# First scale and shift by quarters of the features, and five products begun with them

## The chip, the cores and the metric

One core of a Trainium2 chip runs the whole program. The metric is the device time of one execution in microseconds, as a median of runs; the profile is one execution of its own. The engines are PE (matrix products), PEld (its weight loads), DVE, ACT and POOL (elementwise work), and SP, which issues most of the DMAs here. Each engine takes its own instructions strictly in the order in which they were built.

## The reference, cut to what matters

Two layers of a decoder, for 256 prompt tokens and 8 x 4 sample tokens (288 columns in all), 1024 features: retention, a gated feed-forward part, a gated delta mixer, a second feed-forward part. Before each stands a norm that is scaled and shifted by a vector computed from the condition c. Of all this the change touches the first scale and shift and the first products of retention:

```python
cs = jax.nn.silu(c.astype(jnp.float32))
for l in range(DEPTH):
    mod = cs @ p['w_ada'][l].astype(jnp.float32) + p['b_ada'][l].astype(jnp.float32)
    sh1, sc1, g1, sh2, sc2, g2 = jnp.split(mod, 6, axis=-1)
    h = ada_rmsnorm(x, p['norm_mix'][l], sh1, sc1)
    ...
    out, S = retention_mixer(h, pos0, s_ret[i], p['w_ret_in'][i], p['w_ret_out'][i])

def ada_rmsnorm(x, g, shift, scale):
    xf = x.astype(jnp.float32)
    xn = xf * lax.rsqrt(jnp.mean(xf * xf, axis=-1, keepdims=True) + EPS) * g.astype(jnp.float32)
    return (xn * (1.0 + scale[:, None, :]) + shift[:, None, :]).astype(x.dtype)

def retention_mixer(h, pos0, s0, w_in, w_out):
    proj = jnp.einsum('btd,de->bte', h, w_in).astype(jnp.float32)
    ...
```

## The kernel before, in words

Features lie on partitions: x is 8 tiles (KT) of 128 features by 288 columns. Every product is made exact by splitting: a weight block of 128 x 1024 is loaded raw, ACT casts it to `whi` (line 414), DVE subtracts to get `wlo` (line 415); the normed features are split in the same way into `hh` and `hl`. A product of one output block (`product`, line 533) is then 8 tiles x 3 pairs (whi with hh, whi with hl, wlo with hh), 24 matmuls of 288 columns.

The condition's vectors need `w_ada`, 14 chunks of 8 loads each (512 KB a load). One load is four matmuls into `adaP` (line 453), each with a weight of 32 columns in a quarter of PE's columns. After a chunk's last load ACT copies adaP to `adaev` (line 459), PE transposes that twice into `adaT`, and DVE adds the bias and writes `mod` (line 466). `modulated` (line 601 on) turns mod into features: DVE makes the scale `am` (line 607), the sample columns `hs` in three steps (617, 621, 625), and for each feature tile `h` (631); ACT writes `hh` (626, 632); DVE and POOL write `hl` (634, 627). `rb`, the root of the mean square of each token, comes from PE and DVE beforehand (`token_rsqrt`).

All loads stand in one list, `plan_weights`, and SP issues them in that order as buffers come free: 8 of the pool `more0` and 4 of `raw` in the first phase. At the start the list is chunk 0 (8 loads), one retention weight `wri`, four loads of chunk 1, `wri`, four more, `wri`. Chunk 0 holds shift and scale of the first 512 features, chunk 1 of the others. `first_h` takes chunk 0, makes the first four tiles of features, and begins EARLY = 3 retention products with them, in banks that rotate (`mmt`), chunk 1 between them; the last one (LATE = 1) is begun after the second half's `modulated`. Then the three products get their second half. While `hold` is set, weights of the next phase are not cast. `proj` hands out the begun products first. A scheduling layer orders each engine's instructions, so the code's order is not the order of the program.

`load_cst` loads a table on ACT's queue, behind a POOL copy that reads `mod`, so that it starts no earlier than that column of mod exists.

Of the kernel before, what the change touches and what calls it, by code (L numbers as in the profile page):

```python
# [6 lines left out]
F32 = mybir.dt.float32  # L7
# [3 lines left out]
ALU = mybir.AluOpType  # L11
# [62 lines left out]
EARLY = 3  # L74
LATE = 1
# [115 lines left out]
def lay_out(inp):  # L191
# [8 lines left out]
    wa = np.concatenate([inp["w_ada"][0], inp["w_ada"][1], inp["w_ada_final"]], 1)  # L200

    wa[:, : 2 * DM] = wa[:, : 2 * DM].reshape(DM, 2, 2, 512)[:, ::-1].transpose(0, 2, 1, 3).reshape(DM, 2 * DM)
    d["wada"] = wa.reshape(KT, P, 14, 1024).transpose(2, 0, 1, 3).reshape(14 * KT, P, 1024)
# [90 lines left out]
class Program:  # L294
# [12 lines left out]
    def plan_weights(self):  # L307
        A = self.A
        ada = lambda ch: [("ada", ch, k, A["wada"][ch * KT + k]) for k in range(KT)]
# [12 lines left out]

        second, step = ada(1), -(-KT // (EARLY - LATE))
        plan = [ada(0)]
        for i in range(EARLY):
            plan[0] += wl("wri", i, 1) + second[i * step : (i + 1) * step]
# [120 lines left out]
    def ada_step(self, ch, k, r):  # L447
        nc = self.nc
        if k == 0:
            self.adaP = self.aux("adaP", self.ada_tag)  # L450
        rv = r.rearrange("p (c g f) -> p c g f", c=2, g=4)
# [5 lines left out]
        if k == KT - 1:  # L457
            ev = self.tmp.tile([P, T], F32, tag="t288", name="adaev", bufs=T288)[:, 0:256]
            nc.scalar.copy(ev, self.adaP[:, 0:256])
            pt = self.aux("adaT")  # L460
            for c in range(2):
                nc.tensor.transpose(pt[:, c * P : (c + 1) * P], ev[:, c * P : (c + 1) * P], self.ident)
            pt = pt[:, 0:256].rearrange("p (m r) -> p m r", r=32)[:, :, 0:9]
            for m, m0, n in ((0, 8 + 4 * ch, 4), (4, 4 * ch, 4)) if ch < 2 else ((0, 8 * ch, 8),):
                bias = self.prm("bada")[:, m0 : m0 + n].unsqueeze(2).to_broadcast([P, n, 9])
                nc.vector.tensor_tensor(self.mod[:, m0 : m0 + n, :], pt[:, m : m + n], bias, ALU.add)
# [134 lines left out]
    def modulated(self, norm, sh, sc, name, hi, lo=None, rb=None, m0=0, m1=KT):  # L601

        nc = self.nc
        n, ms = m1 - m0, slice(m0, m1)
# [30 lines left out]
        self.ada_due(FILLS[2])  # L635
# [9 lines left out]
    def first_h(self, rc):  # L645

        nc = self.nc
        h = self.h_tiles("ret")
        self.ada_due(4)
        rb = self.now(self.token_rsqrt(self.ssum, 1.0 / DM, "ret"))  # L650
        self.ada_due()
        self.load_cst(rc, "cst_a", nc.scalar, self.mod[:, 8, 0:1])
        self.modulated(0, 0, 1, "ret", *h, rb, 0, KT // 2)
        begun = []
        self.hold = True
        for i in range(EARLY):
            if i == EARLY - LATE:
                self.ada_due()
                self.modulated(0, 0, 1, "ret", *h, rb, KT // 2, KT)
            w = self.weights("wri")  # L660
            begun.append((self.mmt(f"pe{i}")[:, 0:T], w))
            self.product(*begun[-1], KT, 0, P, h, 0, KT // 2)
        if not LATE:
            self.ada_due()
            self.modulated(0, 0, 1, "ret", *h, rb, KT // 2, KT)
        self.load_cst(rc, "cst_r", nc.scalar, self.mod[:, CST_AT, 0:1])
        self.load_cst(self.cp, "cst_b", nc.scalar, self.mod[:, CST_AT, 0:1])
        self.load_cst(self.cp, "prm_b", nc.scalar, self.mod[:, CST_AT, 0:1])
        for i, (p, w) in enumerate(begun):
            if i == FREE:  # L670
                self.hold = False
            self.product(p, w, KT, 0, P, h, KT // 2)
        self.hold = False
        self.begun = [p for p, _ in begun]
        return h
# [1054 lines left out]
```

## Time and profile before

| what | us |
|---|---|
| median of 3 runs (1228.85 to 1232.32) | 1230.46 |
| the profiled execution's own time | 1235.09 |
| its span | 1233.3 |
| PE busy | 1162.4 |
| DVE busy | 877.2 |
| ACT busy | 608.4 |
| DMA moved, mean 218 GB/s | 269.08 MB |

Mean granted clock of PE over the span: 0.978. The span runs from the first to the last instruction; the execution's own time is 1.8 us longer. Times within the profile are microseconds from the span's start. A matmul's duration runs from its start until its last column is out, and the next one starts before that, so the pace is read from starts or from the chain, not from durations.

### The profile page before, as it was taken

To read this page: it belongs to the slowest core of one execution; us is meant where nothing else is said; L and a number is where in the kernel's file an instruction comes from. 1 tells how busy PE (TensorE), PEld (TensorE's weight loads), DVE (VectorE), ACT (ScalarE), POOL (GpSimd) and SP (SyncE) were. 2 spreads that over 40 slices of the span, in tenths; PEclk is the share of its full clock that TensorE was granted. 3 is DMA by queue.
4 is the path that set the end of the run, shared out by engine and by line. 5 is a ranking of instruction groups with operands and counts; after the bars stand their busy time and mean duration, and the time that the engine had idled before them with its cause. 6 is when DMAs were issued, how large, how long until landed. Compare 5 with 4: busy or idle time off the path is not lost.

```text
span 1233.3 us, 24974 instructions
## 1 busy us (share of the span) xinstructions
PE 1162.4 (94%) x9486; PEld 1045.2 (85%) x9486; DVE 877.2 (71%) x2038; ACT 608.4 (49%) x1258; POOL 326.0 (26%) x504
## 2 busy tenths in 40 slices
PE   6999999999999999999889888988899899999996
PEld 2879788797969999997777777977789699999996
DVE  3657574765766666667769888797965687878785
ACT  2444534344446445543674655745544365555542
POOL 0214142151301221233242124243222212233241
PEclk9999999999999999999989998999999899999997
DMA  9999696866689556556636652534334997878521
GB/s 350 347 335 331 224 338 230 315 239 236 226 298 400 196 161 199 171 181 243 219 84 209 218 165 61 161 129 120 126 109 130 307 358 257 258 238 264 182 76 39
DMA packets 97480, 269.08 MB, mean 218 GB/s; under 512 B 26816, under 2 KB 28832, under 8 KB 97232
## 3 DMA queue, kind: packets, MB, share of 16 engines
q1 hardware_dynamic: 87456, 234.42, 56.6%
q0 software_dynamic: 8032, 29.16, 6.3%
q10 hardware_dynamic: 1872, 3.90, 0.9%
q8 instruction: 75, 1.23, 0.4%
q14 instruction: 45, 0.37, 0.1%
HBM read 236.06 MB, written 31.39 MB: 217 GB/s over the span
## 4 chain that ended last, share of the span: by engine, by line
PE 77%; DVE 13%; ACT 3%; DMA 3%; issue 2%; POOL 1%; ACTq 0%; POOLq 0%; DVEq 0%
PE down L533 17%; PE fg L533 12%; PE fv L533 11%; PE pg L533 4%; PE pv L533 4%; PE adaP L453 4%; PE p L533 3%; PE gv L533 2%; PE gz L533 2%; DVE mp L1319 2%; DVE wlo L415 2%; PE gk L533 2%; PE pO L884 1%; PE pU L903 1%; PE pS L854 1%
## 5 line engine op out<-in xcount | busy, mean ns | idle before, releaser
L415 DVE TENSOR_TENSOR wlo<-more,whi 128x1024 fp32r<-128x1024 f32 x138 | 171.1, 1241 | 80.6 <-ACT whi L414 67.8
L414 ACT CAST whi<-more 128x1024 fp32r<-128x1024 f32 x138 | 144.4, 1048 | 139.6 <-PE down L533 53.3
L414 ACT CAST whi<-raw 128x1024 fp32r<-128x1024 f32 x123 | 128.0, 1044 | 146.3 <-PE down L533 44.1
L415 DVE TENSOR_TENSOR wlo<-raw,whi 128x1024 fp32r<-128x1024 f32 x123 | 154.2, 1256 | 60.6 <-ACT whi L414 36.5
L702 POOL TENSOR_TENSOR x<-x,dt 128x32 f32<-128x32 f32 x159 | 103.1, 649 | 138.9 <-DVE dt L700 137.2
L698 DVE SCALAR_TENSOR_TENSOR x<-down,mod,x 128x256 f32<-128x256 f32 x160 | 76.7, 479 | 52.5 <-PE down L533 51.9
L580 POOL TENSOR_TENSOR fal<-cv,fah 128x288 fp32r<-128x288 f32 x44 | 41.2, 936 | 217.3 <-ACT fah L579 186.3
L533 PE MATMUL down<-fal,whi 128*128 128x288 f32 x352 | 64.5, 295 | 0.0
L533 PE MATMUL down<-fah,whi 128*128 128x288 f32 x352 | 62.2, 294 | 0.0
L533 PE MATMUL down<-fah,wlo 128*128 128x288 f32 x352 | 62.1, 294 | 0.0
L904 DVE SCALAR_TENSOR_TENSOR S<-S,pU 128x512 f32<-128x512 f32 x64 | 42.2, 684 | 24.5 <-PE pU L903 24.4
L533 PE MATMUL fg<-hh_ffn,whi 128*128 128x288 f32 x352 | 58.4, 298 | 0.8 <-ACT hh_ffn L626 0.7
L533 PE MATMUL fv<-hh_ffn,whi 128*128 128x288 f32 x352 | 58.7, 297 | 0.0
L533 PE MATMUL fg<-hh_ffn,wlo 128*128 128x288 f32 x352 | 55.0, 296 | 0.0
L533 PE MATMUL fv<-hh_ffn,wlo 128*128 128x288 f32 x352 | 54.7, 295 | 0.0
L533 PE MATMUL fv<-hl_ffn,whi 128*128 128x288 f32 x352 | 54.2, 295 | 0.0
L533 PEld LDWEIGHTS fg<-hh_ffn,whi 128*128 128x128 f32 x352 | 50.3, 188 | 4.6 <-ACT hh_ffn L632 2.2
L533 PE MATMUL fg<-hl_ffn,whi 128*128 128x288 f32 x352 | 54.0, 295 | 0.0
L533 PEld LDWEIGHTS down<-fal,whi 128*128 128x128 f32 x352 | 52.4, 188 | 0.4 <-issue 0.4
L533 PEld LDWEIGHTS down<-fah,whi 128*128 128x128 f32 x352 | 51.9, 188 | 0.8 <-ACT whi L414 0.8
L533 PEld LDWEIGHTS fv<-hh_ffn,whi 128*128 128x128 f32 x352 | 50.3, 188 | 2.5 <-ACT ftail L934 1.2
L533 PEld LDWEIGHTS down<-fah,wlo 128*128 128x128 f32 x352 | 51.9, 188 | 0.0
(467 smaller groups left out, 2921.3 us busy)
## 6 DMA issues: line engine op xcount, KB each, us to landing
more<-in_wu SPq DMA_DIRECT2D x73, 512.0 KB, 5.2
raw<-in_wada SPq DMA_DIRECT2D x69, 512.0 KB, 4.8
raw<-in_wgi SPq DMA_DIRECT2D x48, 512.0 KB, 3.9
more<-in_wada SPq DMA_DIRECT2D x43, 512.0 KB, 6.3
more<-in_wd SPq DMA_DIRECT2D x36, 512.0 KB, 3.8
S<-in_sr SPq DMA_DIRECT2D x16, 1024.0 KB, 8.5
out_rs<-S POOLq DMA_DIRECT2D x16, 1024.0 KB, 6.9
raw<-in_wri SPq DMA_DIRECT2D x28, 512.0 KB, 4.6
```

The source lines that it names most:

```text
L414: nc.scalar.copy(hi[:, :c], r)
L415: nc.vector.tensor_tensor(lo[:, :c], r, hi[:, :c].bitcast(F32), ALU.subtract)
L453: nc.tensor.matmul(self.adaP[32 * g : 32 * g + 32, 0:256], lhsT=self.cs[:, k, :], rhs=rv[:, :, g, :], start=(k == 0), stop=(k == KT - 1), ...
L533: self.nc.tensor.matmul(out, lhsT=av[:, k, c0 : c0 + m], rhs=b[:, k, :], start=(k0 == 0 and i == 0), stop=(k1 == kts and i == len(seq) - 1))
L580: (nc.gpsimd if pool_lo else nc.vector).tensor_tensor(lo, src, hi.bitcast(F32), ALU.subtract)
L698: nc.vector.scalar_tensor_tensor(xm[:, :TP], p[:, :TP], g[:, 0:1], xm[:, :TP], ALU.mult, ALU.add)
L702: (nc.vector if gate == 11 and last and m == KT - 1 else nc.gpsimd).tensor_tensor(xv, xv, t, ALU.add)
L854: nc.tensor.matmul(pS, lhsT=kt[:, j, c * P : (c + 1) * P], rhs=vt[:, j, :], start=(j == 0), stop=(j == 1))
L884: nc.tensor.matmul(pO4[32 * g : 32 * g + 32, :], lhsT=qm[:, c, 4 * bb + g, :], rhs=S[bb, c][:, g, :], start=(bb == 0 and c == 0), stop=Fal ...
L903: nc.tensor.matmul(pU, lhsT=kms[g][:, c * P : (c + 1) * P], rhs=vst, start=True, stop=True)
L904: nc.vector.scalar_tensor_tensor(S[bb, c][:, g, :], S[bb, c][:, g, :], gamma4, pU, ALU.mult, ALU.add)
L1319: nc.vector.tensor_tensor(m, Ti[:, 0:k, :].rearrange("p j c -> p c j").unsqueeze(1).to_broadcast([P, w, 8, k]), X[:, 0:k, i:k].rearrange(" ...
```

## The change

The first 2048 columns of w_ada are laid out anew, in four quarters of 256 features. A quarter is four loads of 512 KB, each with two of the eight blocks of the contraction, and holds the quarter's shift and scale. A load is now eight matmuls of 128 columns instead of four of 256 (`ada_quarter`), and one transpose follows each quarter instead of two each half. The list of loads is: quarter 0, one `wri`, quarter 1, one, quarter 2, two, quarter 3, one. `first_h` goes by quarters: modulation and two feature tiles of the quarter, then the next two tiles of all products begun so far, then FIRST_W = (1, 1, 2, 1) new products over all tiles there are. Five products are begun instead of three, in five banks named in START_TAGS; the pool of the start holds five split weights instead of three. Bytes and matmul columns stay the same in sum.

```diff
-EARLY = 3
-LATE = 1
+FIRST_W = (1, 1, 2, 1)
+EARLY = sum(FIRST_W)
+START_TAGS = ["c", "mm", "s", "mm", "e"]
...
-    wa[:, : 2 * DM] = wa[:, : 2 * DM].reshape(DM, 2, 2, 512)[:, ::-1].transpose(0, 2, 1, 3).reshape(DM, 2 * DM)
-    d["wada"] = wa.reshape(KT, P, 14, 1024).transpose(2, 0, 1, 3).reshape(14 * KT, P, 1024)
+    d["wada"] = wa[:, 2 * DM :].reshape(KT, P, 12, 1024).transpose(2, 0, 1, 3).reshape(12 * KT, P, 1024)
+    w = wa[:, : 2 * DM].reshape(4, 2, P, 2, 4, 256)[:, :, :, ::-1]
+    d["wadq"] = w.transpose(4, 0, 2, 1, 3, 5).reshape(16, P, 1024)
...
-        second, step = ada(1), -(-KT // (EARLY - LATE))
-        plan = [ada(0)]
-        for i in range(EARLY):
-            plan[0] += wl("wri", i, 1) + second[i * step : (i + 1) * step]
+        plan = [[]]
+        for q, n in enumerate(FIRST_W):
+            plan[0] += [("ada", q - 4, k, A["wadq"][4 * q + k]) for k in range(4)]
+            plan[0] += wl("wri", sum(FIRST_W[:q]), n)
...
+    def ada_quarter(self, q, k, r):
+        nc = self.nc
+        rv = r.rearrange("p (a g f) -> p a g f", a=2, g=4)
+        for a in range(2):
+            for g in range(4):
+                nc.tensor.matmul(
+                    self.adaP[32 * g : 32 * g + 32, 0:P], lhsT=self.cs[:, 2 * k + a, :], rhs=rv[:, a, g, :],
+                    start=(k == 0 and a == 0), stop=(k == 3 and a == 1), skip_group_check=True,
+                )
...
-        self.ada_due(4)
-        rb = self.now(self.token_rsqrt(self.ssum, 1.0 / DM, "ret"))
-        self.ada_due()
-        self.load_cst(rc, "cst_a", nc.scalar, self.mod[:, 8, 0:1])
-        self.modulated(0, 0, 1, "ret", *h, rb, 0, KT // 2)
...
+        for q, n in enumerate(FIRST_W):
             self.ada_due()
-            self.modulated(0, 0, 1, "ret", *h, rb, KT // 2, KT)
...
+            if q == 0:
+                rb = self.now(self.token_rsqrt(self.ssum, 1.0 / DM, "ret"))
+            if q == 2:
+                self.load_cst(rc, "cst_a", nc.scalar, self.mod[:, 2, 0:1])
+            self.modulated(0, 0, 1, "ret", *h, rb, 2 * q, 2 * q + 2)
...
+            for i, (p, w) in enumerate(begun):
+                if q == 3 and i == FREE:
+                    self.hold = False
+                self.product(p, w, KT, 0, P, h, 2 * q, 2 * q + 2)
+            for i in range(n):
+                w = self.weights("wri")
+                begun.append((self.aux(f"pe{len(begun)}", START_TAGS[len(begun)])[:, 0:T], w))
+                self.product(*begun[-1], KT, 0, P, h, 0, 2 * q + 2)
```

The order of the instructions moves on every engine. Three places follow; names are tiles, with a number where it tells two of a kind apart.

DVE, from the last modulation of the start (`mod`) to the first split of features (`hl`). Before:

```order
L466 TENSOR_TENSOR mod<-adaT,prm 128x36 x2
L607 SCALAR_TENSOR_TENSOR am_ret<-mod,prm 128x36
L617 TENSOR_TENSOR hs_ret<-x,am_ret 128x128
L621 TENSOR_TENSOR hs_ret<-hs_ret,rb_ret 128x128
L631 SCALAR_TENSOR_TENSOR h_ret<-x,am_ret,rb_ret 128x256
L415 TENSOR_TENSOR wlo<-more_203,whi 128x1024
L625 TENSOR_TENSOR hs_ret<-hs_ret,mod 128x128
L631 SCALAR_TENSOR_TENSOR h_ret<-x,am_ret,rb_ret 128x256 x3
L634 SCALAR_TENSOR_TENSOR hl_ret<-h_ret,mod,hh_ret 128x256 x4
```

Now, the last quarter:

```order
L491 TENSOR_TENSOR mod<-adaT,prm 128x18 x2
L632 SCALAR_TENSOR_TENSOR am_ret<-mod,prm 128x18
L418 TENSOR_TENSOR wlo<-more_273,whi 128x1024
L642 TENSOR_TENSOR hs_ret<-x,am_ret 128x64
L646 TENSOR_TENSOR hs_ret<-hs_ret,rb_ret 128x64
L656 SCALAR_TENSOR_TENSOR h_ret<-x,am_ret,rb_ret 128x256
L650 TENSOR_TENSOR hs_ret<-hs_ret,mod 128x64
L656 SCALAR_TENSOR_TENSOR h_ret<-x,am_ret,rb_ret 128x256
L418 TENSOR_TENSOR wlo<-more_275,whi 128x1024
L659 SCALAR_TENSOR_TENSOR hl_ret<-h_ret,mod,hh_ret 128x256 x2
```

The last modulation now covers 2 tiles instead of 4; the split of a weight (`wlo`) stands right behind the scale `am`, ahead of the sample columns and of the first tile `h`, where it stood behind the first `h`; that weight, `more_273`, belongs to the next phase.

PE and ACT around the last modulation now (before, twelve matmuls of the third product followed the transpose, and one cast followed the copy `adaev`). PE:

```order
L558 MATMUL pe_437<-hl_ret,whi 128x288 x6
L558 MATMUL pe_437<-hh_ret,wlo 128x288 x6
L479 MATMUL adaP<-more_235,c 32x128 x7
L479 MATMUL adaP<-raw,c 32x128 x8
L479 MATMUL adaP<-more_259,c 32x128 x8
L558 MATMUL pe_556<-hh_ret,whi 128x288 x3
L487 MATMUL adaT<-cst,adaev 128x128
L558 MATMUL pe_556<-hh_ret,whi 128x288 x3
L458 MATMUL adaP<-raw,c 32x256 x4
L558 MATMUL pe_241<-hh_ret,whi 128x288
```

ACT:

```order
L417 CAST whi<-more_269 128x1024
L417 CAST whi<-more_271 128x1024
L485 COPY adaev<-adaP 128x128
L417 CAST whi<-more_273 128x1024
L417 CAST whi<-more_275 128x1024
L657 ACTIVATE hh_ret<-h_ret,mod 128x256
L651 CAST hh_ret<-hs_ret 128x2x32
L657 ACTIVATE hh_ret<-h_ret,mod 128x256
```

The last quarter's loads (`adaP` of 128 columns) come behind the second-quarter parts of four products; six matmuls of the fifth product (`pe_556`), the transpose and the first load of the next chunk (`adaP` of 256 columns) stand before the first matmul on the new tiles (`pe_241`). ACT has two casts of next-phase weights ahead of the copy and two between it and `hh`.

ACT at the start of the first feed-forward part, where `fg` and `fv` are gate and value blocks and `cv` is the gate's convolution. Before:

```order
L932 ACTIVATE cv<-fg_3981,prm_b 128x288
L933 COPY fhalo<-fg_3981 128x32
L934 COPY ftail<-fg_3981 128x2
L414 CAST whi<-raw 128x1024 x2
L932 ACTIVATE cv<-fg_4055,prm_b 128x288
L933 COPY fhalo<-fg_4055 128x32
L934 COPY ftail<-fg_4055 128x2
L414 CAST whi<-more_3953 128x1024
L939 ACTIVATE cv<-cv 128x288 x2
L414 CAST whi<-more_3955 128x1024
```

Now:

```order
L956 ACTIVATE cv<-fg_4073,prm_b 128x288
L957 COPY fhalo<-fg_4073 128x32
L958 COPY ftail<-fg_4073 128x2
L417 CAST whi<-raw 128x1024
L963 ACTIVATE cv<-cv 128x288
L956 ACTIVATE cv<-fg_4147,prm_b 128x288
L957 COPY fhalo<-fg_4147 128x32
L958 COPY ftail<-fg_4147 128x2
L604 CAST fah_4041<-cv 128x288
L417 CAST whi<-more_4043 128x1024
L963 ACTIVATE cv<-cv 128x288
```

The cast of the weight of the second value block was the second of the two `raw` casts, ahead of the second gate block's `cv`; it is now the cast of `more_4043`, behind that block's four ACT instructions and the rounding `fah`.

## Rows read from the trace of the kernel before

**Rows 1.** The page: busy time by engine; shares of the chain that ended last.

```profile
PE 1162.4 (94%) x9486; PEld 1045.2 (85%) x9486; DVE 877.2 (71%) x2038; ACT 608.4 (49%) x1258; POOL 326.0 (26%) x504
...
PE 77%; DVE 13%; ACT 3%; DMA 3%; issue 2%; POOL 1%; ACTq 0%; POOLq 0%; DVEq 0%
```

**Rows 2.** Windows, 46:340 us: busy time (count) by engine, PEclk, DMA share, GB/s.

```profile
46.00:340.00 294.00, 293.89 (x2169) 253.54 (x2169) 186.79 (x332) 129.29 (x223) 85.76 (x104) 1.00 0.77 276
```

**Rows 3.** Timeline of PE: start, us, what, shapes, count [idle before <- releaser].

```profile
11.87 1.08 PE L453 MATMUL adaP<-more,c 128*32 128x256 f32 x8 [0.20 <-DMA more<-in_wada]
13.15 1.06 PE L453 MATMUL adaP<-more,c 128*32 128x256 f32 x2 [0.20 <-DMA more<-in_wada]
14.14 1.44 PE L558 MATMUL st_ret<-ones,ssum 128*128 128x1 f32 x6
...
17.81 1.49 PE L564 MATMUL rb_ret<-cst,tr_ret 128*128 128x128 f32 x6 [0.37 <-DVE tr_ret L550]
...
25.56 0.40 PE L533 MATMUL pe<-hh_ret,whi 128*128 128x288 f32 x1 [2.44 <-ACT hh_ret L626]
...
51.82 1.23 PE L533 MATMUL pv<-hh_ret,whi 128*128 128x288 f32 x8
...
57.42 1.07 PE L453 MATMUL adaP<-raw,c 128*32 128x256 f32 x16
```

**Rows 4.** Windows of the start.

```profile
20.00:52.00 32.00, 27.07 (x202) 19.65 (x195) 21.03 (x45) 12.76 (x20) 5.97 (x11) 0.95 0.92 350
22.80:25.50 2.70, 0.32 (x8) 0.00 (x0) 2.63 (x8) 0.80 (x2) 0.05 (x1) 1.00 0.64 153
26.20:29.50 3.30, 3.30 (x21) 1.26 (x16) 2.64 (x6) 2.15 (x4) 0.00 (x0) 0.50 1.03 415
```

**Rows 5.** Waits of PE, 0:52 us: us in total, times, longest.

```profile
PE adaT L462 <- ACT adaev L459: 1.0, 2, 0.5
...
PE pe L533 <- DVE wlo L415: 0.9, 1, 0.9
PE pe L533 <- ACT whi L414: 0.5, 1, 0.5
```

**Rows 6.** Chain of waits in order of time: start, us, what.

```profile
48.78 4.79 PE pv L533 x36
```

**Rows 7.** Forms by tile: count, ns min/median/max, first and last start us, shapes.

```profile
L453 PE MATMUL adaP<-more,c x96: 379/634/637, 7.9 to 35.4; 128*32 128x256 f32 x96
...
L892 PE MATMUL pO<-vr,ats x32: 272/273/296, 82.6 to 301.1; 128*32 128x128 f32 x32
```

**Rows 8.** Timeline of ACT, start of the program.

```profile
21.23 0.37 ACT L459 COPY adaev<-adaP 128x256 f32<-128x256 f32 x1 [11.95 <-PE adaP L453]
21.50 1.05 ACT L414 CAST whi<-raw 128x1024 fp32r<-128x1024 f32 x1
...
23.88 0.51 ACT L632 ACTIVATE hh_ret<-h_ret,mod 128x256 fp32r<-128x256 f32 x1 [1.33 <-DVE h_ret L631]
```

**Rows 9.** Timeline of DVE, start of the program.

```profile
22.61 0.20 DVE L607 SCALAR_TENSOR_TENSOR am_ret<-mod,prm 128x36 f32<-128x36 f32 x1
...
23.37 0.47 DVE L631 SCALAR_TENSOR_TENSOR h_ret<-x,am_ret,rb_ret 128x256 f32<-128x256 f32 x1
...
38.11 1.22 DVE L415 TENSOR_TENSOR wlo<-more,whi 128x1024 fp32r<-128x1024 f32 x1
```

**Rows 10.** Timeline of SP's queue: the issue of the second retention weight.

```profile
23.19 0.33 SPq L400 DMA_DIRECT2D raw<-in_wri  x1
```

**Rows 11.** Timelines of ACT and PE, start of the first feed-forward part.

```profile
367.10 0.59 ACT L932 ACTIVATE cv<-fg,prm_b 128x288 f32<-128x288 f32 x1 [2.10 <-PE fg L533]
...
367.77 1.05 ACT L414 CAST whi<-more 128x1024 fp32r<-128x1024 f32 x1
...
370.87 0.43 ACT L579 CAST fah<-cv 128x288 fp32r<-128x288 f32 x1
...
367.99 1.32 PE L533 MATMUL fv<-hh_ffn,whi 128*128 128x288 f32 x8
```

More of the change, by code (lines that the diff above doesn't have):

```diff
@@ L308, in plan_weights @@
         A = self.A
-        ada = lambda ch: [("ada", ch, k, A["wada"][ch * KT + k]) for k in range(KT)]
+        ada = lambda ch: [("ada", ch, k, A["wada"][(ch - 2) * KT + k]) for k in range(KT)]
         wl = lambda name, i0, n: [("w", name, 0, A[name][i]) for i in range(i0, i0 + n)]
@@ L450, in ada_step @@
             self.adaP = self.aux("adaP", self.ada_tag)
+        if ch < 0:
+            return self.ada_quarter(ch + 4, k, r)
         rv = r.rearrange("p (c g f) -> p c g f", c=2, g=4)
@@ L463, in ada_step @@
             pt = pt[:, 0:256].rearrange("p (m r) -> p m r", r=32)[:, :, 0:9]
-            for m, m0, n in ((0, 8 + 4 * ch, 4), (4, 4 * ch, 4)) if ch < 2 else ((0, 8 * ch, 8),):
-                bias = self.prm("bada")[:, m0 : m0 + n].unsqueeze(2).to_broadcast([P, n, 9])
-                nc.vector.tensor_tensor(self.mod[:, m0 : m0 + n, :], pt[:, m : m + n], bias, ALU.add)
+            m0, n = 8 * ch, 8
+            bias = self.prm("bada")[:, m0 : m0 + n].unsqueeze(2).to_broadcast([P, n, 9])
+            nc.vector.tensor_tensor(self.mod[:, m0 : m0 + n, :], pt, bias, ALU.add)
+    def ada_quarter(self, q, k, r):
[7 more added lines that the diff above has]
+                )
+        if k == 3:
+            ev = self.tmp.tile([P, T], F32, tag="t288", name="adaev", bufs=T288)[:, 0:P]
+            nc.scalar.copy(ev, self.adaP[:, 0:P])
+            pt = self.aux("adaT")
+            nc.tensor.transpose(pt[:, 0:P], ev, self.ident)
+            pt = pt[:, 0:P].rearrange("p (m r) -> p m r", r=32)[:, :, 0:9]
+            for m, m0 in ((0, 8 + 2 * q), (2, 2 * q)):
+                bias = self.prm("bada")[:, m0 : m0 + 2].unsqueeze(2).to_broadcast([P, 2, 9])
+                nc.vector.tensor_tensor(self.mod[:, m0 : m0 + 2, :], pt[:, m : m + 2], bias, ALU.add)
     def spawn(self, gen):
@@ L603, in modulated @@
         nc = self.nc
-        n, ms = m1 - m0, slice(m0, m1)
+        n, ms, rb_given = m1 - m0, slice(m0, m1), rb
         am = self.tmp.tile([P, KT, 9], F32, tag="am", name=f"am_{name}", bufs=2)[:, 0:n]
@@ L634, in modulated @@
                 nc.vector.scalar_tensor_tensor(lo[:, m, :TP], h, shift[:, i, 0:1], hi[:, m, :TP].bitcast(F32), ALU.add, ALU.subtract)
-        self.ada_due(FILLS[2])
+        if rb_given is None:
+            self.ada_due(FILLS[2])
     def h_tiles(self, name):
@@ L648, in first_h @@
         h = self.h_tiles("ret")
-        self.ada_due(4)
-        rb = self.now(self.token_rsqrt(self.ssum, 1.0 / DM, "ret"))
-        self.ada_due()
-        self.load_cst(rc, "cst_a", nc.scalar, self.mod[:, 8, 0:1])
-        self.modulated(0, 0, 1, "ret", *h, rb, 0, KT // 2)
         begun = []
         self.hold = True
-        for i in range(EARLY):
-            if i == EARLY - LATE:
-                self.ada_due()
-                self.modulated(0, 0, 1, "ret", *h, rb, KT // 2, KT)
[L660 to L663, printed above, removed]
-            self.ada_due()
[L665 to L672, printed above, removed]
+        rb = None
+        for q, n in enumerate(FIRST_W):
+            self.ada_due()
+            if q == 0:
[3 more added lines that the diff above has]
+            self.modulated(0, 0, 1, "ret", *h, rb, 2 * q, 2 * q + 2)
+            if q == 3:
+                self.load_cst(rc, "cst_r", nc.scalar, self.mod[:, CST_AT, 0:1])
+                self.load_cst(self.cp, "cst_b", nc.scalar, self.mod[:, CST_AT, 0:1])
+                self.load_cst(self.cp, "prm_b", nc.scalar, self.mod[:, CST_AT, 0:1])
+            for i, (p, w) in enumerate(begun):
[6 more added lines that the diff above has]
+                self.product(*begun[-1], KT, 0, P, h, 0, 2 * q + 2)
         self.hold = False
```

## The prediction

> **What bounds the kernel now.** I read the page's totals and chain first: PE is busy 94% of the span and is 77% of the chain that ended last [rows 1]. The windows say where it is not: between 46 and 340 us PE stands still for 294.00 - 293.89 = 0.11 us [rows 2]. Whatever the start loses or gains therefore reaches 340 us undiminished, and the question is when PE gets there with the same work behind it. The change rewrites the first 50 us, so I read PE's timeline there. Two points matter: PE's first product on the normed features, at 25.56, and 51.82, when five products (two of the query, two of the key, one of the value of head 0) and all sixteen modulation loads are done [rows 3]. Between 20 and 52 PE is busy 27.07 of 32.00 us [rows 4]; most of the missing 4.93 us stands in five waits: 2.44 for the first half's features [rows 3], 1.0 for the copies of the two halves' modulation, 0.5 for a weight's cast and 0.9 for a wlo, both in the second half [rows 5]. DMA is full there (share 0.92) [rows 4], but PE's last wait for a load ends at 13.15 [rows 3]: from there on the order of ACT, DVE and PE bounds, not the loads.
>
> **The change, step by step.** Prices at full clock: a fp32r product of 288 columns 0.133 us (36 in 4.79) [rows 6], a modulation load 0.5 us (16 records, two loads, in 1.07) [rows 3].
>
> *A load in eight products of 128 columns instead of four of 256.* The trace has no such product of adaP. Bounds: the same time, since the columns are the same in sum, or twice it, if each product cost as much as a wide one: 1.0 us, 4.5 us more over the nine loads that fall after PE's first product. The nearest row is pO<-vr,ats, the same 32 x 128 shape: 273 ns from start to end against 379 for 256 columns, so the columns carry the difference [rows 7]. I take 0.5 us.
>
> *The first quarter.* Its fourth load is read out at 11.87 + 1.08 = 12.95 [rows 3]. ACT now has the cast of the first retention weight ahead of the copy of adaP; that weight is the fifth load, and the fifth load of before is first read at 13.15 [rows 3]. So: cast 1.05 to 14.2, copy 0.37 to 14.6 [rows 8], one transpose at the start's slow clock some 0.35 to 14.95, the token sums 1.44 to 16.4, the root 2.23 (from 15.58 to 17.81 before) [rows 3] with two small DVE steps of 0.2 between to 19.0, its broadcast 1.49 to 20.5 [rows 3], the small step and one tile 0.2 + 0.47, the rounding 0.5 [rows 8, 9]. PE's first product comes at 21.7 instead of 25.56.
>
> *What PE still has to do.* Before, from 25.56: seven loads 3.5, two transposes 0.44, 120 products 16.0: 19.9 us. It took 51.82 - 25.56 = 26.26. Of the 6.3 us more, the three waits of the second half are 1.9 (half of the 1.0, 0.5 and 0.9) [rows 5]; the stretch 26.20 to 29.50 ran at a granted clock of 0.50, after one in which PE was busy 0.32 of 2.70 us [rows 4], and lost half of 3.3, 1.65; 2.8 us are short stops and changes of weights. Now, from 21.7: nine loads 4.5, three transposes 0.7, the same 120 products 16.0, and one load of the next modulation chunk that the order now has ahead of the end, 0.5: 21.7 us.
>
> *PE's waits.* They come from ACT and DVE taking their work in order.
> Quarter 1: the second weight's cast stands behind the copy (0.37 + 1.05); PE has three products and a transpose, 0.6: it waits 0.8. The features' second tile stands behind a wlo of 1.22 [rows 9]; PE has four products and two loads: 1.1.
> Quarter 2: 0.6 for copy and transpose, 0.9 and 0.35 for the casts of the third and fourth weight, which stand behind the copy one after the other, 1.0 for the features, which stand behind both casts: 2.85.
> Quarter 3: this is the largest. Copy 0.37, transpose 0.3, two additions and the scale 0.5: 1.2. Then DVE's row is a wlo of a weight of the next phase, whose cast ACT starts only after the copy: it can start at 0.37 + 1.05 = 1.45 and ends at 2.7. Two small steps 0.4, a tile 0.47, its rounding 0.5: 4.1 us from the last load to PE's first product on the last two tiles. PE has six products of the fifth block, the transpose and that one load, 1.45: it waits 2.7.
> After the last product the next one takes the bank of the first, and waits until DVE has read that twice: 0.5.
> Sum 8.0 us (0.8 + 1.1 + 2.85 + 2.7 + 0.5 = 7.95), against 1.9 before.
>
> *Sum at the start.* 21.7 + 21.7 + 8.0 + the same 2.8 of short stops + 1.65 if a stretch runs at half clock as before = 55.9, or 54.2 without. Before it is 51.82 + 0.5 for the same work, 52.3. So 3.6 us later, or 1.9. I take the half clock, since two of the waits, 0.8 and 1.1, fall where it fell before. The Trainium skill (TensorE: Matmul & The Clock Gate, the section on the HAM clock gate) says that slow is the default state and that activity releases it; no run here shows yet whether products from 21.7 on are enough. By that rule PE's earlier start would keep the full clock and the sum at the start would be 1.9; the granted clock of before agrees in this, that it fell behind the idle stretch and rose again behind the busy one [rows 4].
>
> *Loads.* Bytes are the same. The fifteenth load waits until PE has read the ninth, at about 23.9; before, the fourteenth waited until 23.19 [rows 10], so from there on the queue is one load further than it was. At 1.28 us a load (11.87 to 13.15) [rows 3] the last quarter's four are in by some 36, an estimate from that step and the issue. The tables behind cst_r now go out after quarter 2, beside the last weights; I cost them at nothing, because PE reads the last quarter's loads only behind quarter 2's products, at about 45. If that cover is gone, the cast that holds the wlo in quarter 3 is late next.
>
> *Further on.* The sixth product takes another bank than before, and so the builder's order shifts throughout retention; with 0.11 us of idle time there I cost that at nothing. At the start of the first feed-forward part the shift is seen: the cast of the second value block now stands behind everything that ACT does with the second gate block. That block's end lets cv start at 367.10; cv and two copies take until 367.77, the rounding fah 0.43, the cast 1.05 [rows 11]: the value block can start at 369.3. Before it started at 367.99, right behind two loads [rows 11]. PE loses 1.3 us; no later row differs.
>
> **Forecast.** 3.6 + 1.3 = 4.9 us slower. The profiled execution would come from 1235.09 to 1240.0 and the median of 1230.46 to 1235.4; the profiled one stands 4.6 above the median, and I carry the difference over. A measurement here can tell some 0.3%, 3.7 us, from no change.
>
> **Rivals.**
> *The early start pays (faster).* Had PE no waits at the quarters and no half clock, five products would be done at 21.7 + 21.7 + 2.8 = 46.2, 6.1 ahead of 52.3; with 1.3 lost later that is 1225.7. For it: the last part after the modulation shrinks from 84 products (36 + 48) to 42. Against it: the waits are queue positions, not speeds. It decides where the waits sum to under 1.1 us (3.7 faster) instead of 8.0; it breaks even at 4.8.
> *The clock stays full (no change that can be told).* 1.9 + 1.3 = 3.2: 1233.7. The same result comes if the waits are a fifth shorter than I make them.
> *The clock falls once more (slower still).* The wait of 2.7 us in quarter 3 resembles the one of 2.44 that a half-clock stretch followed. One more such stretch loses 1.65: 4.9 + 1.65 = 6.6, 1237.1.
> *The change doesn't begin five products with the quarters.* The order shows that it does; no chance of its own.
>
> **Chances.** Forecast 0.52, of which 0.42 beyond 3.7 us; clock falls again 0.13; clock stays full or waits somewhat shorter 0.26; early start pays 0.09. That makes faster 0.09, same 0.36, slower 0.55. The range goes from 1230.5, which takes in the second rival with three of the eight us of waits gone, to 1239.5, which takes in the third and half of the narrow products' upper bound.
>
> **What would show it.** In the new profile: PE's first product near 21.7; adaP's loads at 0.5 us at full clock; the longest wait of the start, 2 us or more, before the first product of quarter 3, near 50, with DVE's wlo ahead of the small steps; the fifth block's end near 55; idle time between 20 and 56 of 8 to 9 us against 4.93 in 20 to 52; then no idle time up to the feed-forward part, and there a wait of about 1.3 us for a cast before the second value block. The prediction is wrong if quarter 3's features are ready before 46, if the loads of a quarter take 1 us each, or if PE waits for weights in retention.

## The result, and the profile after

The changed kernel takes 1245.49 us (median of 4 runs, 1239.15 to 1248.71), the kernel before 1231.39 us (median of 4): ratio 1.0094, with a 95% interval from 1.0068 to 1.0119. The direction was forecast; the size, 4.9 us, was not: some 11.6 us are lost (0.0094 x 1231.39; the two medians lie 14.1 apart), and the median lies above the upper end of the stated range, 1239.5.

The profiled execution of the changed kernel is the fastest of its four (1239.15 us, span 1237.4). So its end says little. I therefore compare places in the program. PE's timelines of the two kernels, at the first product behind the start, the first product of the first feed-forward part, and its first `down`; of before:

```profile
351.81 0.40 PE L533 MATMUL fg<-hh_ffn,whi 128*128 128x288 f32 x1 [0.73 <-ACT hh_ffn L626]
...
409.67 0.29 PE L533 MATMUL down<-fah,whi 128*128 128x288 f32 x1
```

and of the changed kernel:

```profile
60.49 0.80 PE L558 MATMUL pv<-hh_ret,whi 128*128 128x288 f32 x4 [0.34 <-DVE rt L755]
...
363.25 0.40 PE L558 MATMUL fg<-hh_ffn,whi 128*128 128x288 f32 x1 [1.17 <-ACT hh_ffn L651]
...
422.33 0.42 PE L558 MATMUL down<-fah,whi 128*128 128x288 f32 x2
```

Behind the start, with five products and two loads of the next chunk done, it stands at 60.49 against 51.82 + 2 x 0.5 [rows 3] = 52.8: 7.7 us late. At the first feed-forward part it is 11.44 late, at its first `down` 12.66, and at the first product of the next layer still so (595.73 against 583.07). Three losses, then: **7.7 at the start, 3.8 in retention, 1.2 in the feed-forward part.** Only the last was as forecast. These are places in one execution of each kernel. (Later the execution profiled of before lost more time to a lower clock: 0.95 granted from 800 to 900 us against 1.00 after. That is a difference between two executions, not between the kernels; the runs' ratio agrees with 12.66 and not with the 4.1 between the two profiled times.)

**The start.** PE's timeline after:

```profile
12.04 1.08 PE L479 MATMUL adaP<-more,c 128*32 128x128 f32 x16 [0.20 <-DMA more<-in_wadq]
...
21.27 0.61 PE L558 MATMUL pe<-hh_ret,whi 128*128 128x288 f32 x1
...
22.80 0.45 PE L558 MATMUL pe<-hl_ret,whi 128*128 128x288 f32 x1
...
28.06 0.85 PE L558 MATMUL pe<-hh_ret,whi 128*128 128x288 f32 x2 [1.00 <-ACT hh_ret L651]
28.84 1.08 PE L479 MATMUL adaP<-raw,c 128*32 128x128 f32 x16
...
37.99 1.06 PE L558 MATMUL pe<-hh_ret,whi 128*128 128x288 f32 x6 [0.57 <-ACT hh_ret L657]
...
40.26 0.29 PE L558 MATMUL pe<-hl_ret,whi 128*128 128x288 f32 x1
...
43.91 0.53 PE L479 MATMUL adaP<-more,c 128*32 128x128 f32 x11
...
45.94 0.64 PE L558 MATMUL pe<-hh_ret,whi 128*128 128x288 f32 x3
51.13 1.08 PE L458 MATMUL adaP<-raw,c 128*32 128x256 f32 x8 [4.55 <-DMA raw<-in_wada]
52.15 2.77 PE L558 MATMUL pe<-hh_ret,whi 128*128 128x288 f32 x10
```

Two things stand here that the forecast did not have. First, the long wait before the last quarter's products is 4.55 us, and what ends it is not a feature but a load: the first of the *next* modulation chunk, which the order has ahead of those products. Second, look at the lengths. A product alone takes 0.45 us at 22.80 and 0.29 at 40.26; the sixteen records of a load take about 1.0 us at 28.84 (to 29.85), as they did at 12.04, and 0.5 behind 43.91 (46 records, nearly three loads, to 45.35). So PE runs at half its clock from the start of the program until some 32 us. The granted clock does not show this stretch: in this trace its records begin with the first change, at 31.87, and what lies ahead is printed as 1.00:

```profile
21.00:31.00 10.00, 8.85 (x64) 5.40 (x63) 4.81 (x14) 3.10 (x8) 0.99 (x3) 1.00 0.90 343
33.00:46.00 13.00, 11.30 (x150) 9.61 (x142) 7.34 (x14) 5.67 (x9) 1.84 (x4) 1.00 0.76 281
49.00:55.70 6.70, 4.57 (x23) 3.79 (x24) 3.88 (x9) 1.66 (x4) 1.09 (x1) 0.50 1.03 417
```

(windows of the changed kernel; the third number from the end is the granted clock). The 1.00 of the first window is not a measurement, as the products' lengths show; the 0.50 of the last is on record, behind the long wait. Before, one stretch of 0.50 was on record, from 26.2 to 29.5 [rows 4]. That kernel too began at half clock (one load in 1.08 us at 11.87 [rows 3]), but its first record, a rise, stands at 22.7, ahead of its first product on the features at 25.56.

The list of PE's waits from 12 to 62 us, as in [rows 5] before, gives the rest:

```profile
PE adaP L458 <- DMA raw<-in_wada: 4.6, 1, 4.6
PE adaT L487 <- ACT adaev L485: 1.9, 2, 1.4
PE pe L558 <- ACT hh_ret L651: 1.0, 1, 1.0
PE pe L558 <- ACT whi L417: 0.6, 1, 0.6
PE pe L558 <- ACT hh_ret L657: 0.6, 1, 0.6
```

(1.4 of the 1.9 for adaev lies ahead of the first product.) In the shares of the chain that ended last, DMA has gone from 3% [rows 1] to 5% and PE from 77% to 73%:

```profile
PE 73%; DVE 14%; DMA 5%; ACT 4%; issue 3%; POOL 1%; SPq 0%; ACTq 0%; POOLq 0%; DVEq 0%
```

**Why the load was late.** SP's queue, which issues the loads:

```profile
32.56 0.38 SPq L403 DMA_DIRECT2D more<-in_wadq  x1
32.99 0.90 SPq L403 DMA_DIRECT2D more<-in_wri  x2
...
43.62 0.81 SPq L403 DMA_DIRECT2D more<-in_wri  x2
44.52 0.86 SPq L403 DMA_DIRECT2D raw<-in_wada  x2
```

It stands still from 33.9 to 43.6, and the waits of that queue (30 to 62 us) say for what:

```profile
SPq L403 <- DMA cst_r<-in_cst_r: 9.7, 1, 9.7
...
SPq L403 <- DMA cst_a<-in_cst_a: 6.5, 1, 6.5
```

The table cst_r goes out on ACT's queue at 35.23 and lands 8.4 us later. In the order of the program with its waits, each DMA issue of SP and ACT takes the next of eight completion semaphores in turn; the third weight of the next phase (`more1_273`) has the same one as cst_r (both carry number 106 in the trace), so SP waits for the table, with the modulation load queued behind. A wait of the same kind, 6.5 us for cst_a, had held SP before, until 32.1. The order:

```
24 L403 DMA more1_273<-in_wri 128x1024 [waits DMAHW6_49]
25 L403 DMA more1_275<-in_wri 128x1024 [waits DMAHW7_49]
26 L403 DMA raw_321<-in_wada 128x1024 [waits DMAHW0_49,DVE_49]
```

Before, cst_r went out later (37.30) and held SP for 7.9 us. But there the two modulation loads stand ahead of the weight that shares its semaphore, and were issued before the wait:

```profile
31.23 1.47 SPq L400 DMA_DIRECT2D raw<-in_wada  x2
36.19 1.63 SPq L400 DMA_DIRECT2D raw<-in_wri  x2
45.74 0.80 SPq L400 DMA_DIRECT2D more<-in_wri  x2
```

The wait is of the same kind; what is queued behind it is not.

### The profile page after: what moved, and what is told of

The parts are those of the page before. It is cut to its first block, busy times and chain, and to the rows that moved or that the text cites. A ratio compares the mean times of both kernels' runs of the same rounds, so it can differ in the third digit from the quotient of the medians.

```text
span 1237.4 us, 25247 instructions
## 1 busy us (share of the span) xinstructions
PE 1161.6 (94%) x9614; PEld 1048.3 (85%) x9614; DVE 882.0 (71%) x2050; ACT 608.7 (49%) x1262; POOL 322.1 (26%) x506
## 4 chain that ended last, share of the span: by engine, by line
PE 73%; DVE 14%; DMA 5%; ACT 4%; issue 3%; POOL 1%; SPq 0%; ACTq 0%; POOLq 0%; DVEq 0%
PE down L558 16%; PE fg L558 12%; PE fv L558 11%; PE pg L558 4%; PE pv L558 4%; PE p L558 3%; PE adaP L458 3%; DVE mp L1343 3%; DVE wlo L418 2%; PE gv L558 2%; PE gk L558 2%; PE pU L927 2%; PE pO L908 1%; DVE Ti L1347 1%; PE gz L558 1%
## 5 line engine op out<-in xcount | busy, mean ns | idle before, releaser
L418 DVE TENSOR_TENSOR wlo<-more,whi 128x1024 fp32r<-128x1024 f32 x139 | 174.8, 1258 | 90.1 <-ACT whi L417 75.6
L418 DVE TENSOR_TENSOR wlo<-raw,whi 128x1024 fp32r<-128x1024 f32 (+1 forms) x122 | 153.0, 1256 | 59.5 <-ACT whi L417 31.3
L417 ACT CAST whi<-raw 128x1024 fp32r<-128x1024 f32 (+1 forms) x122 | 127.1, 1043 | 136.9 <-PE down L558 48.2
```

Of the source, the lines that this page charges most:

```text
L417: nc.scalar.copy(hi[:, :c], r)
L418: nc.vector.tensor_tensor(lo[:, :c], r, hi[:, :c].bitcast(F32), ALU.subtract)
```

## The experiments

**Theory A** says that the loss has separate causes, the load behind the table, the turn of the banks that moves retention's order, the half clock at the start, and the later cast in the feed-forward part. The rival of each run stands in its expectation. "Late by" below is against the profile of before, at the same three places as above; ratios are against runs of before on the same chip. A "late by" compares one execution with one, and the clock at the start differs between executions: experiment 7, whose order on PE is that of before throughout the start, came out of it 1.16 us later. A ratio takes in all runs.

**1. Quarters alone.** Diff against the changed kernel:

```diff
-FIRST_W = (1, 1, 2, 1)
+FIRST_W = (1, 1, 1, 0)
...
         self.begun = [p for p, _ in begun]
+        self.n_mm = 3
```

> The changed kernel with quarters but only three products begun (FIRST_W 1, 1, 1, 0) and the count that picks the banks set to 3, as before: from the middle of the first head on its order is that of the kernel before. Theory A (most of the start's loss is the quarters' waits, and what is lost after 60 us comes from beginning five): later than before by 3 to 8 us at 70 us, and by the same within 0.5 us at 600 us; ratio 1.003 to 1.006. Rival (quarters lose nothing by themselves, beginning five does): within 1 us of before at 70 us, ratio 0.999 to 1.001.

Ratio 1.0031 [1.0015, 1.0048]. Late by 3.87 us at the first feed-forward part and by the same 3.87 at its first `down`. Theory A holds: quarters cost at the start and nowhere else.

**2. Five products alone.** Diff against the kernel before:

```diff
-EARLY = 3
+EARLY = 5
+START_TAGS = ["c", "mm", "s", "mm", "e"]
...
-            begun.append((self.mmt(f"pe{i}")[:, 0:T], w))
+            begun.append((self.aux(f"pe{i}", START_TAGS[i])[:, 0:T], w))
```

> The kernel before, with its two halves, but five products begun in the changed kernel's banks; behind the start PE's order is the changed kernel's, row for row. Theory A (the changed order costs 4 us between 70 and 340 us, where PE never stands still for long, and the later cast 1.2 us at the first feed-forward part): within 1.5 us of before at 70 us, 4 us later by 340 us, 5 us by 600 us; ratio 1.003 to 1.006. Rival (the growth after 70 us is an aftermath of the disturbed start, of loads that come late): no growth between 70 and 340 us, only the 1.2 us; ratio 1.000 to 1.002.

Ratio 1.0059 [1.0037, 1.0080]. Late by 2.2 us behind the start (55.01 against 52.8; 1.5 was the bound; its half clock lasts from 25.0 to 31.8), 6.99 at the feed-forward part, 8.17 at its `down`. So 4.8 us are lost in retention though this start has no quarters, and the rival falls. With experiment 1, by these profiles: 3.87 + 8.17 = 12.04 of the 12.66.

**3. The banks as before.** Diff against the changed kernel:

```diff
         self.begun = [p for p, _ in begun]
+        self.n_mm = 5
```

> The changed kernel with the count that picks the banks of the products set to 5 behind the start, so that from the sixth product on each takes the bank that it has before. Theory A (the 4 us between 70 and 340 us come from the banks' turn, which moves small products next to each other): 7 us later than before at 70 us as the change is, but no more than 8 at 340 us and 9 at 600 us; ratio 1.006. Rival (they come from the places of the modulation loads, which this edit leaves): 11 us at 340 us as the change is, ratio 1.009.

Ratio 1.0074 [1.0055, 1.0094]. Late by 6.3 us behind the start, 7.36 at the feed-forward part, 8.55 at its `down`: retention loses 1.1 us instead of 3.8, as theory A has it. The same stretch, from the first product behind the start to the feed-forward part, as windows; before, changed, five alone, banks as before:

```profile
52.80:351.80 299.00, 296.71 (x2222) 253.17 (x2221) 188.79 (x351) 130.53 (x228) 82.59 (x104) 1.00 0.77 276
```

```profile
60.50:363.20 302.70, 300.28 (x2212) 254.42 (x2212) 195.27 (x357) 129.84 (x228) 82.40 (x107) 1.00 0.77 269
```

```profile
55.00:358.80 303.80, 300.94 (x2214) 254.47 (x2212) 195.23 (x357) 129.67 (x228) 81.95 (x107) 1.00 0.78 271
```

```profile
59.10:359.10 300.00, 297.29 (x2212) 253.85 (x2212) 190.69 (x355) 130.38 (x228) 84.99 (x107) 1.00 0.77 270
```

PE does not stand still longer: 2.3 to 2.9 us in all four. With the turn of the banks as before it is *busy* 297.29 us; in the two other kernels with 2212 records, 300.28 and 300.94, 3.0 and 3.7 us longer. The 0.11 us of idle time [rows 2], on which the prediction rested here, could not show this loss.

**4. The tables on POOL's queue.** Diff against the changed kernel, the same for cst_a, cst_b and prm_b:

```diff
-                self.load_cst(rc, "cst_r", nc.scalar, self.mod[:, CST_AT, 0:1])
+                self.load_cst(rc, "cst_r", nc.gpsimd, self.mod[:, CST_AT, 0:1])
```

> The changed kernel with the four tables (cst_a, cst_r, cst_b, prm_b) issued from POOL's queue instead of ACT's, at the same place and with as many bytes; the loads of SP's queue then share no completion semaphore with them. Theory A (SP stood 9.7 us for the landing of cst_r, and so the modulation load that PE awaits went out at 44.5 us instead of some 37): PE's wait before the last quarter's features falls from 4.6 to 2 to 3 us and ends on features, not on a load; 2 us less lost at 70 us (5 instead of 7), 3.5 if the half clock behind the wait goes too; ratio 1.006 to 1.008. Rival (the load is late because the engines are full with the tables' bytes, whoever waits): PE still waits 4 us or more for that load, ratio 1.009 as the change is.

In the profile theory A holds. SP issues the loads in the order of the changed kernel and stands for no table:

```profile
30.39 2.35 SPq L403 DMA_DIRECT2D raw<-in_wada  x2
```

PE's timeline at the last quarter reads

```profile
47.33 0.64 PE L458 MATMUL adaP<-raw,c 128*32 128x256 f32 x8
50.48 1.60 PE L558 MATMUL pe<-hh_ret,whi 128*128 128x288 f32 x10 [2.50 <-ACT hh_ret L651]
...
55.13 1.22 PE L558 MATMUL pe<-hh_ret,wlo 128*128 128x288 f32 x8
56.28 0.64 PE L458 MATMUL adaP<-raw,c 128*32 128x256 f32 x8
```

The wait is 2.50 us, ends on a feature, and no half clock follows it (a product alone, 0.29 at 52.89). Behind it, at 57.27, it is 3.2 us ahead of the changed kernel and 9.73 late at the feed-forward part's `down`. DVE stands as forecast, the wlo of a next-phase weight ahead of the features' small steps:

```profile
47.65 0.18 DVE L632 SCALAR_TENSOR_TENSOR am_ret<-mod,prm 128x18 f32<-128x18 f32 x1
47.74 1.22 DVE L418 TENSOR_TENSOR wlo<-more,whi 128x1024 fp32r<-128x1024 f32 x1
48.88 0.22 DVE L642 TENSOR_TENSOR hs_ret<-x,am_ret 128x64 f32<-128x64 f32 x1
```

The runs do not separate it from the change: ratio 1.0089 [1.0068, 1.0111], the rival's 1.009 and not the 1.006 to 1.008 of theory A. The wait's cause is shown, with both tables' waits taken away at once; that the kernel gains 3 us of 1231 by it is not shown by the runs.

**5. Tables and banks.** Both diffs, 3 and 4.

> The changed kernel with both edits: the four tables on POOL's queue and the count of the banks as before. Theory A (the two costs lie in different places and add up): of the 12.65 us that the change is behind at 600 us, 3.2 go with the load's wait (as with the tables alone) and 4 with the banks, 5.4 are left: about 4 at 70 us, 4.5 at 340, 5.5 at 600; ratio 1.004. Rival (the two overlap: with the banks restored PE waits elsewhere for what the tables hold up): 7 us or more at 600 us, ratio 1.006 or above.

Ratio 1.0074 [1.0046, 1.0103]. Late by 9.4 us behind the start, 9.88 and 11.09 later. Retention loses 0.5 us and the feed-forward part 1.2, as theory A has it; no load is waited for. But the start is worse by 4.95 us than in experiment 4 (62.22 against 57.27), with the same order on PE. The windows of this profile show why:

```profile
16.50:33.50 17.00, 14.41 (x108) 10.36 (x108) 7.00 (x24) 3.53 (x8) 1.70 (x4) 0.50 0.98 379
37.00:43.70 6.70, 5.70 (x34) 4.96 (x35) 5.50 (x8) 3.48 (x6) 2.32 (x3) 0.50 1.02 410
54.10:57.40 3.30, 3.30 (x16) 3.30 (x15) 0.92 (x3) 0.00 (x0) 0.24 (x1) 0.50 0.87 304
```

In experiment 4 the half clock lasted until 32.1 and did not come back. Here half of the 5.70 and of the 3.30 busy us is lost on top, 4.5 us. So in this profile the forecast of 5.4 fails at the clock. The rival's numbers came (11.09 and 1.0074, against 7 or more and 1.006 or above), but not its mechanism, another wait of PE's for what the tables hold up.

**6 and 7. The banks alone, in the kernel before.** Two kernels, three products begun as before:

```diff
         self.begun = [p for p, _ in begun]
+        self.n_mm = 2
```

and the same with 5.

> The kernel before, three products begun, with only the count of the banks set back by one behind the start, which is the changed kernel's turn of the banks from the sixth product on. Theory A (the turn alone costs the 4 us): equal to before at 70 us, 3 to 5 us later at 340 us, the same at 600 us; ratio 1.002 to 1.004. Rival (the cost needs the five products, by the places of the modulation loads behind them): under 1 us at 340 us, ratio 0.999 to 1.001.

> The kernel before with the count of the banks put forward by two. Theory A says that the turn of the banks sets the time between 70 and 340 us, not in which direction: a change of 1 us or more in that stretch, either way, and nothing at the start. Rival: no change, ratio 0.999 to 1.001.

With 2: ratio 1.0048 [1.0032, 1.0064], late by 5.01 us at the feed-forward part (356.82 against 351.81), and by no more afterwards. With 5: ratio 1.0007 [0.9991, 1.0024], late by 1.16 (352.97), all of it at the start, where both profiles run at half clock from 25 to some 31.7 us and before did so from 26.2 to 29.5 [rows 4]. The difference, 3.85 us, is the turn of the banks alone, and the runs agree: 1.0048 less 1.0007 is 5.1 us, with intervals that do not overlap. Theory A holds in 6; in 7 its guess that any other turn changes the time was wrong. PE's windows over the same work, from 60 us in the kernel before,

```profile
60.00:342.00 282.00, 281.89 (x2073) 242.27 (x2072) 178.15 (x319) 125.03 (x215) 79.35 (x98) 1.00 0.77 274
```

and in 6:

```profile
62.20:347.00 284.80, 284.59 (x2071) 243.21 (x2071) 181.89 (x318) 124.54 (x215) 76.76 (x98) 1.00 0.77 269
```

Again PE is busy all the time, and 2.7 us longer with as many records (2071 against 2073). Part of it can be placed. From each start to the next start on PE, the 32 products `pS<-vt,kt` of retention take 11.26 us in sum in the kernel before and 12.46 in experiment 6, and the 64 of `pO<-at,vt` 9.41 and 10.05: 1.84 of the 2.7 us. The other traces fall in line: 12.46 and 10.05 in the changed kernel and in experiments 2, 4 and 9, whose banks are turned by one, and 11.26 and 9.41 to 9.49 in 1, 3, 5, 8, 10, 11 and 12, whose banks are as before. Experiment 7, turned by two, has 11.57 and 8.59. Why the same products take longer there, and where the rest of the loss lies, is open.

**8. Quarters with three products, tables on POOL's queue.** Diffs 1 and 4.

> Quarters with three products begun, banks as before, and the four tables on POOL's queue. Theory A (of the 3.9 us that quarters alone cost, the wait of 1.6 us for a load comes from the tables and goes): 2 to 2.5 us later than before at 70 us and at 600 us, PE waits for no load before the last quarter's features; ratio 1.002. Rival (the features are as late as the load and take its place): 3.5 to 4 us as without, ratio 1.003.

Ratio 1.0022 [1.0001, 1.0043]; late by 3.09 us at the feed-forward part and 3.10 at its `down`, no load waited for. The load's wait is gone; the time lies between the two expectations, and the runs cannot tell it from experiment 1.

**9 to 12. The clock.** PE's first waits filled with products that do no work of the kernel and go to a bank that nothing reads:

```diff
+        if k == 3 and q == 0:
+            pf = self.aux("pfill", "e")
+            for i in range(FILLERS):
+                g = i % 4
+                nc.tensor.matmul(
+                    pf[32 * g : 32 * g + 32, 0:P], lhsT=self.cs[:, 2 * k, :], rhs=rv[:, 0, g, :], ...
+                )
         if k == 3:
```

with FILLERS = 10: in the changed kernel (9), in the kernel of 5 (10), in the kernel of 8 (11). In the kernel before (12), eight transposes of adaev behind the first half's own two.

> The changed kernel with ten extra products of the first quarter's fourth load, into a bank that nothing reads, in PE's wait for the first copy of adaP (13.1 to 14.6 us). They need some 1.4 us at half clock and do no work of the kernel. Theory A (PE's products run at half clock until 31.9 us, 0.44 us against 0.29, and this is the 5 us that the sum of the start lacked; the first idle stretch is what keeps the clock down): the first rise on record comes at 20 to 25 us instead of 31.9, five products are done 2 to 5 us earlier unless the wait for the table takes it back; with that wait left 1 to 4 us less behind at 70 us; ratio 1.006 to 1.009. Rival (the clock's first rise does not depend on this stretch): rise at 31 to 32 us as in three of the profiles with quarters, ratio 1.0094.

Ratio 1.0098 [1.0072, 1.0124]: a miss. The clock rose early, at 13.8 us (the first product takes 0.40 us at 20.26, where it took 0.61 in the changed kernel), and fell again; the windows:

```profile
14.00:20.50 6.50, 3.99 (x68) 3.06 (x64) 4.70 (x21) 1.53 (x5) 0.21 (x1) 1.00 1.02 406
20.60:30.80 10.20, 9.06 (x66) 6.13 (x66) 4.25 (x12) 2.49 (x6) 0.68 (x3) 0.50 0.97 367
```

Behind a stretch in which PE was busy 3.99 of 6.50 us it ran at half clock from 20.6 to 30.8, where the changed kernel had done so until 32. The load's wait was 4.9, and a half-clock stretch at 362 us added to the loss (14.95 late at the first `down`).

> The changed kernel with the tables on POOL's queue, the count of the banks as before, and the ten extra products. Theory A (three separate costs: the load's wait 3.2, the banks 4, the clock up to 5): 1 to 4 us behind before at 600 us, of which 1.2 at the first feed-forward part; ratio 1.001 to 1.003. Rival (the waits of the quarters grow by what the clock gives back, since ACT and DVE set the pace): 5 us behind as the sum of the first two alone gives, ratio 1.004.

Ratio 1.0074 [1.0053, 1.0095]; late by 3.9 us behind the start, 4.61 and 5.78 later. In this profile that is the rival's 5 us, with a half-clock stretch as in 9 (20.3 to 30.5): the first two edits add up, and the third bought nothing beyond them. The runs do not bear this out. Their ratio is that of experiments 3 and 5, 9.1 us, and the lower end of the interval, 6.5, lies above the 5 us. So that the two edits add up is not shown.

> Quarters with three products begun, banks as before, tables on POOL's queue, and the ten extra products. Theory A: of the 2.4 to 3.1 us that this is behind without the extra products, most goes with the clock: between 1 us ahead and 1.5 us behind before at 70 and at 600 us; ratio 0.999 to 1.001. Rival (pace set by ACT and DVE): 2 to 3 us behind, ratio 1.002.

Here the clock rose at 14.8 us and was half again from 18.3 to 21.6 us only:

```profile
18.30:21.60 3.30, 3.30 (x33) 2.37 (x32) 2.09 (x6) 1.05 (x3) 0.48 (x1) 0.50 1.03 406
21.70:45.00 23.30, 17.23 (x220) 13.03 (x213) 12.95 (x34) 9.09 (x17) 4.70 (x11) 1.00 1.01 397
```

The kernel is 0.89 us *ahead* of before at the feed-forward part, 4.0 ahead of experiment 8, whose order it has but for the extra products. The ratio is 1.0013 [0.9997, 1.0028], no difference from before. In the profiles theory A holds, and the half clock at the start is worth some 4 us; the runs' ratios, 1.0022 in experiment 8 and 1.0013 here, do not separate the two kernels. It has the lowest ratio of the kernels with quarters, and it does not beat the kernel before.

> The kernel before with eight extra transposes of the first half's adaev, into a bank that nothing reads, in PE's wait for the first half's features (23.1 to 25.6 us). Theory A (the half-clock stretch behind that wait, 3.4 us in one profile and 6.8 in three others, comes from PE standing still there): no half clock between 24 and 32 us, 1 to 3 us ahead of before at 70 us and at 600 us; ratio 0.998 to 0.999. Rival (the extra work delays the loads or the clock falls all the same): no gain, ratio 1.000 or above.

Ratio 1.0005 [0.9989, 1.0022], late by 0.03: a miss. The half clock near 26 us was gone and one from 39.1 to 42.4 had come, behind 13.6 us in which PE was busy 11.05. The first rise came later too, at 25.4 us against 22.7 before (a load still takes 1.08 us at 24.10):

```profile
25.40:39.00 13.60, 11.05 (x90) 6.40 (x90) 6.33 (x15) 4.00 (x7) 1.01 (x4) 1.00 0.95 365
39.10:42.40 3.30, 3.26 (x13) 3.27 (x14) 3.03 (x8) 2.68 (x6) 0.47 (x1) 0.50 1.05 420
```

So filling one wait does not hold the clock. What decides its rise and fall within the first 60 us was not settled: kernels with the same order of PE at the start differed between executions. In the three profiles with quarters and extra products the first rise is on record at 13.5 to 14.8 us; in the six without, at 12.7 (experiment 1), 13.1 (5), 22.1 (3) and 31.9 to 32.1 (the changed kernel, 4 and 8). So the extra products are not shown to have caused the early rise, and the loss of the changed kernel's first stretch may belong to the execution as much as to the change.

## Why the prediction was right and wrong

The direction was right. Of the 12.66 us in the profiles 4.9 were forecast, and the 7.8 that are lacking stand in two places: 4.1 at the start (7.7 against 3.6) and 3.8 in retention (against nothing). The steps that failed are the clock's term, mis-sized; the order in retention, put at nothing; and the tables in "Loads", put at nothing, which cost a wait and part of the clock's loss.

**The first quarter: right.** First product at 21.27 (21.7 forecast).

**The narrow load: right.** 0.5 us at full clock (46 records, nearly three loads, in 1.44 us), neither dearer nor cheaper than a wide one.

**PE's waits: the sum right by luck, the largest one's cause wrong.** 7.74 us from the first product to 60.49, against 8.0: the first two quarters fell 2.15 us short and the third ran 1.85 over. Quarter 1 was 1.0 instead of 1.9, quarter 2 was 1.6 instead of 2.85, the bank 0.34 instead of 0.5. Quarter 3 was 4.55 instead of 2.7, and not for its features. The step that failed here is "Loads": "The tables behind cst_r now go out after quarter 2 ...; I cost them at nothing, because PE reads the last quarter's loads only behind quarter 2's products". That held for the last quarter's loads (the last landed at 38.7, and PE read them from 43.91), and cst_r went out no later than before; but the sum itself counts "one load of the next modulation chunk that the order now has ahead of the end", at 0.5 us of work, and I did not ask when *that* one is issued. It now stands behind the weight that shares its semaphore with cst_r, where before it stood ahead (experiment 4: with the tables elsewhere the wait is 2.50, close to my 2.7, and where I put it).

**The clock: mis-sized.** "1.65 if a stretch runs at half clock as before". I carried the one stretch of [rows 4] over. In the changed kernel PE ran at half clock from before the first product at 21.27 until some 32 us, and again from 49 to 55.7. Of the first stretch, from that product on, 10.6 us less 1.1 idle at half clock lose 4.7; of the second, 4.57 busy lose 2.3. With these 7.0 in place of 1.65, and the measured 7.74 of waits in place of 8.0, the sum comes to 21.27 + 22.2 (the work and a second load) + 2.8 + 7.74 + 7.0 = 61.0, against 60.49 measured. The rival "The clock stays full" had the opposite sign of what came. The prediction knew the slow clock of the start ("one transpose at the start's slow clock"), but took it to have ended by PE's first product, as it had before. Of the rule that I cited from the Trainium skill (TensorE: Matmul & The Clock Gate, the section on the HAM clock gate: slow is the default, activity releases it) the first half agrees with this trace, which is at half clock from its start to 31.87. The second half, as I used it, does not: PE was busy 8.85 of 10.00 us from 21 to 31, and the clock stayed at half. What released it at 31.87, and not earlier, is open. "The clock falls once more", 0.13, came as well, behind the load's wait; experiment 4, without that wait, has no such stretch.

**The order in retention: wrong.** "With 0.11 us of idle time there I cost that at nothing". It cost 3.8 us in the change, 4.8 with five products alone and 3.85 with the banks alone, without idle time. That PE is busy says that it always has an instruction, not that each instruction takes as long in another order.

**The feed-forward part: right.** 1.2 us (1.3 forecast), and only where five products begin:

```profile
378.46 1.07 PE L458 MATMUL adaP<-raw,c 128*32 128x256 f32 x16
380.63 1.33 PE L558 MATMUL fv<-hh_ffn,whi 128*128 128x288 f32 x8 [1.09 <-ACT whi L417]
```

The second value block waits for its cast, which stands behind the second gate block's work on ACT; before, it followed two loads directly [rows 11].

**The early start does not pay.** The condition of the rival at 0.09, waits under 1.1 us, did not come: PE waited 7.74. The nearest to it that I reached, quarters with three products and a short half clock, ends level with before (experiment 11), and there, by the list of waits, PE still stands 3.9 us for features.

## What to carry to other kernels

When loads change places, read the issuing queue's own waits: a transfer of another queue can hold it through a shared completion semaphore, and a load that has slid from ahead of that wait to behind it can be late by the whole of it (issued at 44.52 here, at 30.39 without the tables' waits). Where an engine has no idle time, a changed order can still cost it time: compare busy time over the same instructions, not idle time. And check the clock by the length of one known product before trusting a granted clock of 1.00 near the start of a trace.

## What I had not expected of the hardware

The order of the same products and loads on PE, moved only by which bank each product takes, changed PE's busy time in retention by 2.7 us of 282 (experiment 6). The clock at the start differs between executions of kernels whose PE has the same order there: the changed kernel and experiment 3 share it up to 60 us, and a product alone takes 0.45 us at 22.80 in the first and 0.29 at 22.48 in the other. Experiment 3 came to its wait for the load at 43.8, 2.8 us ahead of the changed kernel, and waited 5.94 there, until 49.71: a load that is late takes back what the clock gave.
